# Updating the recurrent state of six heads behind the first output tiles of a two-layer step

## The chip, the cores and the metric

The kernel runs on one core of a Trainium2 chip. A core has five engines with an instruction queue each: TensorE (PE in the rows, with its weight loads as PEld), VectorE (DVE), ScalarE (ACT), GpSimd (POOL) and SyncE (SP, which here only issues DMAs). They are ordered among each other by semaphores. The metric is the device time of one launch in microseconds, the median of several runs.

## The reference

One step of a two-layer trunk for 256 prompt tokens and 8 sample tokens (each a sequence of its own with one new token). The first layer is sliding-window attention, the second a gated linear recurrence (HGRN2) with 12 heads of 128 x 128; both have four heads of attention on a memory, a gate, an output projection and a LayerNorm. What the change touches is the state of the sample tokens in the second layer, `state_hgrn`. With one token a sequence, the recurrence comes down to this, for each sample and head:

```python
fg = lb + (1.0 - lb) * sigmoid(f)      # 128 numbers, one per row of the state
k  = 1.0 - fg
state_new = fg[:, None] * state + k[:, None] * v[None, :]
o = q @ state_new                       # then RMS norm, gate, output projection
```

Both `o` and `state_new` are results: `o` feeds the rest of the layer, `state_new` is only stored (8 samples x 128 x 128 in float32, 512 KB a head).

## The kernel before

Tokens stand in columns, T = 264 of them (256 prompt, 8 sample). All large operands come through one list of **units**, built by `stream.add` and run by `Stream.run` (L58 to L131). A unit is one load of up to 128 x 2048 float32 (1 MB) on SP into a buffer `raw`, a split of it into two float16 parts `hl`, and a function that uses the split. The first part is rounded by ACT (L97), the remainder is made by DVE (L98), and every product is three PE passes (`passes`, L302 to L305). There are four `raw` and four `hl` buffers, used in turn; a unit's load waits until the raw slot that it takes has been released, its split until an hl slot has been. The last eight output tiles have hl buffers of their own, `held`, and are multiplied in two goes: first 176 columns, later the other 88.

For the second layer the list holds, for each pair of heads `pi`, the projections f and v of both heads, and then for each head the projection q, the state (`state_unit`) and, for the first eight heads, the gate (`early_gate`). Then come four projections `mq` for the memory's queries, four units of cached memory keys (`ck_unit`), four of cached memory values (`cv_unit`) with the gates 8 to 15 between them, and the sixteen tiles of the output weight `w_o` (`out_unit`). Gates 14 and 15 are the last two before the tiles. The prompt's recurrence (`hg_side`) and its memory attention (`memp_side`) are run in pieces between the units; the last head pair's norm (L1183, L1186) needs a logarithm and an exponential, with a load of ACT's tables ahead of each.

`state_unit(h)` computes o for the eight samples from the split state. It then updates the state in place in its raw slot: `sel` selects the value row of each sample on PE (`vb`, L1233), ACT scales the state by the forget gate (L1237), DVE adds the outer product (L1238), 8 of each for a head, and POOL issues the store (L1241). The unit is added with `whole=True`, so its raw slot stays taken until the unit is done, and the next load into it waits for the store.

A scheduler fixes the order on each engine; the order in which the functions are called is its input.

Of the kernel before, what the change touches and what calls it, by code (L numbers as in the profile page):

```python
# [18 lines left out]
P = 128  # L19
# [12 lines left out]
NM = 4  # L32
HD = 12
NG1 = 8
SW = 1024.0
SA = 8.0
SP = 1024.0
# [7 lines left out]
RMS_EPS = 1e-6  # L45
HALVES = ((0, slice(0, 64), slice(64, P)), (1, slice(64, P), slice(0, 64)))
LEVELS = (1, 2, 4, 8, 16, 32, 64)
NMASK = (len(LEVELS) - 1) * 64

SM_LB = 0  # L50
# [7 lines left out]
class Stream:  # L58
# [11 lines left out]

    def parts(self, i):
        n = 4 if i == 0 else 2 if i < 4 else 1
        w = self.units[i][0].shape[1] // n
        return [slice(k * w, (k + 1) * w) for k in range(n)]

    def load(self, i):
        t = self.pool.tile([P, 2048], F32, tag="raw", name=f"raw{i}", bufs=self.nraw)
        for k, s in enumerate(self.parts(i)):
            self.nc.sync.dma_start(t[:, s], self.units[i][0][:, s])
            if i < 4:  # L80
                self.after_load(i, k)
        self.raw[i] = t
# [52 lines left out]
def trunk_kernel(  # L135
# [73 lines left out]
    l_t = cp.tile([24, 383], F32, tag="ms", name="l_t", bufs=2)  # L209
    l_d = dp.tile([24, LROW], F32, name="l_d")[:, :]  # L210
    bias_s = pm.tile([P, 2, NQ], F32, name="bias_s")

    def small_work():
        with ExitStack() as behind:
# [695 lines left out]
    def wb(w, i):  # L910
        return w[i].rearrange("p c f -> p (c f)")
# [111 lines left out]
    def hv_unit(h):  # L1023
        def fn(hl):
            p1 = H["p"]
            i = h % 2
            pt = proj(hl, xhl, T, f"hv{h}")
            if i == 0:
                cur["vn"] = p1.tile([P, 2, 2, P], F32, tag="vn", name=f"vn{h}", bufs=2)
                cur["vr"] = p1.tile([P, 2, P], F16, tag="vr", name=f"vr{h}", bufs=2)  # L1030
                cur["vt"] = p1.tile([P, 2, T], F32, tag="vt", name=f"hvt{h}", bufs=1)
            vt = cur["vt"][:, i]
            vs = H["vs"][i]
            nc.scalar.activation(vt, pt, AF.Copy, scale=CP)
            split_from(vs[:, :TS], vs[:, TS : 2 * TS], pt[:, TP:T], 1.0 / SW)
            vn, vr = cur["vn"], cur["vr"]
            later.append(lambda: hv_rows(h, vt, vs, vn, vr))

        return fn

    def hv_rows(h, vt, vs, vn, vr):
        i = h % 2
        pt = bank("pt", 2, f"hvp{h}")
        for c in range(2):
            nc.tensor.transpose(pt[:, c * P : (c + 1) * P], vt[:, c * P : (c + 1) * P], ident)
        nc.scalar.activation(vn[:, i].rearrange("p c v -> p (c v)"), pt[:, :256], AF.Copy)
        p16 = ps.tile([P, P], F16, tag="pt", name=f"hvr{h}", bufs=2)
        nc.tensor.transpose(p16, vs, ident16)
        nc.vector.tensor_copy(vr[:, i], p16)

    def early_gate(j):
        def fn(hl):
# [11 lines left out]
    def hg_side(pi, q, vn, fg, qk):  # L1064
# [129 lines left out]
            done[1].add(h)  # L1194
        yield

    def state_unit(h):
        def fn(hl):
            p1 = H["p"]
            pi, i = h // 2, h % 2  # L1200
            raw = stream.raw[state_at[h]][:, : TS * P]
            R = raw.rearrange("p (b v) -> p b v", b=TS)
            v = hl[:, :, : TS * P].rearrange("p s (b v) -> p s b v", b=TS)
            vr, fgs, ks8 = cur["vr"][:, i], cur["fg"][:, i, TP:T], cur["ks8"][:, i]
            qs, vts = (cur[n][:, i, TP:T] for n in ("q", "vt"))
            ks = cur["kk"][:, i]
            if i == 0:
                osb[pi] = p1.tile([P, 2, T], F32, tag="osb", name=f"osb{pi}", bufs=2)
            qk = p1.tile([P, TS], F32, tag="qk", name=f"qk{h}", bufs=2)
            qf = p1.tile([P, TS], F32, tag="qf", name=f"qf{h}", bufs=2)  # L1210
            qfh = p1.tile([P, TS, 2], F16, tag="qfh", name=f"qfh{h}", bufs=2)
            nc.vector.scalar_tensor_tensor(qf, qs, SA * 0.5 * CP, fgs, op0=ALU.mult, op1=ALU.mult)
            nc.vector.scalar_tensor_tensor(qk, qs, 8.0 * 0.5 * CP / SK, ks, op0=ALU.mult, op1=ALU.mult)
            qkh = p1.tile([P, 2, TS], F16, tag="qkh", name=f"qkh{h}", bufs=2)
            nc.scalar.activation(qkh[:, 0], qk, AF.Copy)
            nc.vector.tensor_tensor(qkh[:, 1], qk, qkh[:, 0], op=ALU.subtract)
            nc.scalar.activation(qfh[:, :, 0], qf, AF.Copy)
            nc.vector.tensor_tensor(qfh[:, :, 1], qf, qfh[:, :, 0], op=ALU.subtract)
            po = bank("ms", 1, f"hos{h}")
            pov = po[:, : 2 * TS].rearrange("p (b s) -> p b s", s=2)  # L1220
            for b in range(TS):
                mm(pov[:, b], v[:, 0, b], qfh[:, b], start=True, stop=False)
                mm(pov[:, b, 0:1], v[:, 1, b], qfh[:, b, 0:1], start=False, stop=True)
            pq = po[:, 2 * TS : 3 * TS]
            for s in range(2):
                mm(pq, H["ones"], qkh[:, s], start=s == 0, stop=s == 1)
            nc.vector.tensor_reduce(qf, pov, axis=AX.X, op=ALU.add)
            nc.vector.tensor_tensor(qk, pq, vts, op=ALU.mult)
            nc.vector.scalar_tensor_tensor(osb[pi][:, i, TP:T], qf, 1.0 / (SA * SA), qk, op0=ALU.mult, op1=ALU.add)
            for g in range(2):  # L1230
                pvb = bank("pt", 2, f"vb{h}{g}")
                for bb in range(4):
                    mm(pvb[:, bb * P : (bb + 1) * P], H["sel"][:, 4 * g + bb], vr, start=True, stop=True)  # L1233
                for bb in range(4):
                    b = 4 * g + bb
                    s = R[:, b]
                    nc.scalar.activation(s, s, AF.Copy, scale=fgs[:, b : b + 1])  # L1237
                    nc.vector.scalar_tensor_tensor(  # L1238
                        s, pvb[:, bb * P : (bb + 1) * P], ks8[:, b : b + 1], s, op0=ALU.mult, op1=ALU.add
                    )  # L1240
            nc.gpsimd.dma_start(ss_o[pi, :, i * TS * P : (i + 1) * TS * P], raw)  # L1241

        return fn

    state_at = {}
    for pi in range(HD // 2):
        for part, unit in (("f", f_unit), ("v", hv_unit)):
            for i in range(2):
                stream.add(wb(w_in1, NB1[part] + 2 * pi + i), unit(2 * pi + i))
        for h in (2 * pi, 2 * pi + 1):  # L1250
            stream.add(wb(w_in1, NB1["q"] + h), hq_unit(h))
            state_at[h] = len(stream.units)
            stream.add(state[pi][:, (h % 2) * TS * P : (h % 2 + 1) * TS * P], state_unit(h), SA, whole=True)
            if h < NG1:
                stream.add(wb(w_in1, NB1["g"] + h), early_gate(h))
    for h in range(NM):
# [17 lines left out]
        g1(late.popleft())  # L1274
    for i in range(NC):
        stream.add(wb(w_o[1], i), out_unit(1, i), home=hold if i >= NC - NSPLIT else None)

    def after(i):
        if i == 1:
# [153 lines left out]
```

## Time and profile before

| | us |
|---|---|
| median of 3 runs | 905.26 |
| fastest and slowest | 904.99, 907.28 |
| profiled execution | 906.08 |
| its span in the profile | 904.3 |
| PE busy in the span | 886.6 |
| DVE busy | 701.5 |
| ACT busy | 582.4 |

The span runs from the first to the last recorded instruction; 1.78 us of the profiled execution lie around it. Busy times count instructions as they occupy an engine; transfers are not in them.

### The profile page before, as it was taken

Reading aid. Unit: us, or ns where it says so; the run is one execution under the profiler, and the core shown is the slowest. Engines: PE = TensorE matmul, PEld = TensorE weight load, DVE = VectorE, ACT = ScalarE, POOL = GpSimd, SP = SyncE. Lnnn points to the kernel's source line nnn. Section 1 sums busy time; section 2 is a strip of 40 time slices with the busy share of each in tenths; the row PEclk is TensorE's granted clock in tenths of the full one; section 3 lists DMA queues with packets and bytes.
Section 4 is the critical chain, followed back from the end, with each engine's and each line's share of the span. In section 5 each row is a group of like instructions: output and inputs, shape, how many; then the busy total and the mean of one; then the engine's idle time right before and its main releaser. Section 6 shows DMA issues by size and latency. Waiting matters only on the chain.

```text
span 904.3 us, 21814 instructions
## 1 busy us (share of the span) xinstructions
PE 886.6 (98%) x9281; PEld 762.9 (84%) x9281; DVE 701.5 (78%) x1230; ACT 582.4 (64%) x982; POOL 34.9 (4%) x68
## 2 busy tenths in 40 slices
PE   9999999999999999999999999999999999799996
PEld 6888889678888888876888888898888888688996
DVE  6879877669886666697687887979788989678736
ACT  6767776657664444476766877777777585858415
POOL 1100010000000000002000000000000000000000
PEclk9999999999999999999999999999999999899999
DMA  9998566557785555556374655827454878456303
GB/s 340 392 353 317 188 245 209 188 208 265 262 333 192 187 192 203 207 198 214 127 292 137 216 201 174 299 101 260 160 215 164 303 283 308 172 207 244 130 2 97
DMA packets 37853, 198.67 MB, mean 220 GB/s; under 512 B 4555, under 2 KB 10732, under 8 KB 17532
## 3 DMA queue, kind: packets, MB, share of 16 engines
q1 hardware_dynamic: 33024, 181.55, 56.3%
q0 software_dynamic: 4688, 15.67, 4.6%
q8 instruction: 72, 1.18, 0.5%
q14 instruction: 25, 0.20, 0.1%
q10 hardware_dynamic: 44, 0.07, 0.0%
HBM read 180.03 MB, written 17.22 MB: 218 GB/s over the span
## 4 chain that ended last, share of the span: by engine, by line
PE 77%; DVE 8%; ACT 6%; DMA 6%; issue 3%; SPq 0%; ACTq 0%; DVEq 0%
PE o L303 5%; PE o L305 5%; PE o L304 5%; PE g L305 5%; PE g L303 5%; PE g L304 5%; DVE hl L98 4%; ACT hl L97 2%; PE hv L305 2%; PE hv L303 2%; PE hv L304 2%; DMA raw<-in_w_in 2%; PE hq L303 2%; PE hq L305 2%; PE hq L304 2%
## 5 line engine op out<-in xcount | busy, mean ns | idle before, releaser
L98 DVE SCALAR_TENSOR_TENSOR hl<-raw,hl 128x2048 f16<-128x2048 f32 (+2 forms) x168 | 358.6, 2138 | 82.0 <-ACT hl L97 81.0
L97 ACT ACTIVATE hl<-raw 128x2048 f16<-128x2048 f32 (+2 forms) x168 | 299.2, 1784 | 97.8 <-PE o L305 45.4
L305 PEld LDWEIGHTS <-hl 128*128 128x128 f16 (+2 forms) x2048 | 197.4, 98 | 31.8 <-DVE hl L98 2.9
L303 PEld LDWEIGHTS <-hl 128*128 128x128 f16 (+2 forms) x2048 | 197.3, 98 | 30.6 <-issue 2.2
L304 PEld LDWEIGHTS <-hl 128*128 128x128 f16 (+2 forms) x2048 | 197.4, 98 | 30.3 <-issue 2.2
L305 PE MATMUL g<-xhl,hl 128*128 128x264 f16 x512 | 142.0, 277 | 2.4 <-DVE hl L98 2.4
L303 PE MATMUL g<-xhl,hl 128*128 128x264 f16 x512 | 141.9, 277 | 0.0
L304 PE MATMUL g<-xhl,hl 128*128 128x264 f16 x512 | 141.9, 277 | 0.0
L303 PE MATMUL o<-mix,hl 128*128 128x264 f16 x384 | 105.4, 276 | 0.8 <-DVE xres L747 0.8
L304 PE MATMUL o<-mix,hl 128*128 128x264 f16 x384 | 105.8, 276 | 0.0
L305 PE MATMUL o<-mix,hl 128*128 128x264 f16 x384 | 105.7, 276 | 0.0
L303 PE MATMUL q<-xhl,hl 128*128 128x264 f16 x192 | 53.0, 276 | 1.0 <-DVE kst L251 1.0
L303 PE MATMUL f<-xhl,hl 128*128 128x264 f16 x192 | 52.9, 276 | 0.4 <-DVE mvhl L251 0.4
L305 PE MATMUL hv<-xhl,hl 128*128 128x264 f16 x192 | 53.0, 276 | 0.0
L303 PE MATMUL hq<-xhl,hl 128*128 128x264 f16 x192 | 53.0, 276 | 0.0
L304 PE MATMUL hq<-xhl,hl 128*128 128x264 f16 x192 | 53.0, 276 | 0.0
L305 PE MATMUL hq<-xhl,hl 128*128 128x264 f16 x192 | 53.0, 276 | 0.0
L304 PE MATMUL hv<-xhl,hl 128*128 128x264 f16 x192 | 53.0, 276 | 0.0
L303 PE MATMUL hv<-xhl,hl 128*128 128x264 f16 x192 | 53.0, 276 | 0.0
L304 PE MATMUL q<-xhl,hl 128*128 128x264 f16 x192 | 53.0, 276 | 0.0
L305 PE MATMUL q<-xhl,hl 128*128 128x264 f16 x192 | 53.0, 276 | 0.0
L304 PE MATMUL f<-xhl,hl 128*128 128x264 f16 x192 | 52.9, 276 | 0.0
(338 smaller groups left out, 1858.4 us busy)
## 6 DMA issues: line engine op xcount, KB each, us to landing
raw<-in_w_in SPq DMA_DIRECT2D x88, 1024.0 KB, 6.4
raw<-in_w_o SPq DMA_DIRECT2D x32, 1024.0 KB, 5.0
raw<-in_w_mk SPq DMA_DIRECT2D x8, 1024.0 KB, 4.9
raw<-in_w_mv SPq DMA_DIRECT2D x8, 1024.0 KB, 4.9
raw<-in_c_mk SPq DMA_DIRECT2D x8, 1024.0 KB, 5.1
raw<-in_c_mv SPq DMA_DIRECT2D x8, 1024.0 KB, 7.0
raw<-in_state SPq DMA_DIRECT2D x12, 512.0 KB, 5.4
out_ss<-raw POOLq DMA_DIRECT2D x12, 512.0 KB, 5.5
```

Source lines behind the costliest of these rows:

```text
L97: hi = self.nc.scalar.activation(hl[:, 0, s], raw[:, s], AF.Copy, scale=scale)
L98: lo = self.nc.vector.scalar_tensor_tensor(hl[:, 1, s], raw[:, s], scale, hl[:, 0, s], op0=ALU.mult, op1=ALU.subtract)
L303: mm(out, lhs(0), rhs(0), start=start, stop=False)
L304: mm(out, lhs(0), rhs(1), start=False, stop=False)
L305: return mm(out, lhs(1), rhs(0), start=False, stop=stop)
```

## The change

The six heads of `LATER`, 6 to 11, leave their state alone in `state_unit`. Its end copies the forget gate and the scaled k of the eight samples behind the value rows in one small tile (`vr`, now 128 x 80 numbers a head) and stores it to DRAM, and the unit no longer keeps its raw slot. The update itself stands in new units, `update_unit(h)`, one behind each of the output tiles 0, 2, 4, 6, 8 and 10. Such a unit loads the state a second time, loads the small tile behind it into the same raw slot, is not split, and does the scales, sums and the store. The selector is loaded a second time, once, into a buffer that the memory softmax also uses. Nothing else changes.

```diff
--- before.py
+++ after.py
@@ -32,6 +32,7 @@
 NM = 4
 HD = 12
 NG1 = 8
+LATER = tuple(range(6, HD))
 SW = 1024.0
 SA = 8.0
 SP = 1024.0
@@ -45,6 +46,7 @@
 RMS_EPS = 1e-6
 HALVES = ((0, slice(0, 64), slice(64, P)), (1, slice(64, P), slice(0, 64)))
 LEVELS = (1, 2, 4, 8, 16, 32, 64)
+KEPT = P // 2 + 2 * TS
 NMASK = (len(LEVELS) - 1) * 64
 
 SM_LB = 0
@@ -70,12 +72,19 @@
 
     def parts(self, i):
         n = 4 if i == 0 else 2 if i < 4 else 1
-        w = self.units[i][0].shape[1] // n
+        src = self.units[i][0]
+        if isinstance(src, list):
+            return [None]
+        w = src.shape[1] // n
         return [slice(k * w, (k + 1) * w) for k in range(n)]
 
     def load(self, i):
         t = self.pool.tile([P, 2048], F32, tag="raw", name=f"raw{i}", bufs=self.nraw)
         for k, s in enumerate(self.parts(i)):
+            if s is None:
+                for home, src in self.units[i][0]:
+                    self.nc.sync.dma_start(home(t), src)
+                continue
             self.nc.sync.dma_start(t[:, s], self.units[i][0][:, s])
             if i < 4:
                 self.after_load(i, k)
@@ -209,6 +218,7 @@
     l_t = cp.tile([24, 383], F32, tag="ms", name="l_t", bufs=2)
     l_d = dp.tile([24, LROW], F32, name="l_d")[:, :]
     bias_s = pm.tile([P, 2, NQ], F32, name="bias_s")
+    kept = {pi: dp.tile([P, 2, KEPT], F32, name=f"kept{pi}") for pi in sorted({h // 2 for h in LATER})}
 
     def small_work():
         with ExitStack() as behind:
@@ -1027,7 +1037,7 @@
             pt = proj(hl, xhl, T, f"hv{h}")
             if i == 0:
                 cur["vn"] = p1.tile([P, 2, 2, P], F32, tag="vn", name=f"vn{h}", bufs=2)
-                cur["vr"] = p1.tile([P, 2, P], F16, tag="vr", name=f"vr{h}", bufs=2)
+                cur["vr"] = p1.tile([P, 2, KEPT], F32, tag="vr", name=f"vr{h}", bufs=2)
                 cur["vt"] = p1.tile([P, 2, T], F32, tag="vt", name=f"hvt{h}", bufs=1)
             vt = cur["vt"][:, i]
             vs = H["vs"][i]
@@ -1046,7 +1056,7 @@
         nc.scalar.activation(vn[:, i].rearrange("p c v -> p (c v)"), pt[:, :256], AF.Copy)
         p16 = ps.tile([P, P], F16, tag="pt", name=f"hvr{h}", bufs=2)
         nc.tensor.transpose(p16, vs, ident16)
-        nc.vector.tensor_copy(vr[:, i], p16)
+        nc.vector.tensor_copy(vr[:, i, : P // 2].bitcast(F16), p16)
 
     def early_gate(j):
         def fn(hl):
@@ -1194,6 +1204,33 @@
             done[1].add(h)
         yield
 
+    def update(h, R, vr, fgs, ks8, sel):
+        for g in range(2):
+            pvb = bank("pt", 2, f"vb{h}{g}")
+            for bb in range(4):
+                mm(pvb[:, bb * P : (bb + 1) * P], sel[:, 4 * g + bb], vr, start=True, stop=True)
+            for bb in range(4):
+                b = 4 * g + bb
+                s = R[:, b]
+                nc.scalar.activation(s, s, AF.Copy, scale=fgs[:, b : b + 1])
+                nc.vector.scalar_tensor_tensor(
+                    s, pvb[:, bb * P : (bb + 1) * P], ks8[:, b : b + 1], s, op0=ALU.mult, op1=ALU.add
+                )
+        nc.gpsimd.dma_start(ss_o[h // 2, :, h % 2 * TS * P : (h % 2 + 1) * TS * P], R.rearrange("p b v -> p (b v)"))
+
+    late_sel = []
+
+    def update_unit(h):
+        def fn(raw):
+            if not late_sel:
+                late_sel.append(cp.tile([P, TS, P], F16, tag="ms", name="late_sel", bufs=2))
+                nc.sync.dma_start(late_sel[0], sel_d)
+            R = raw[:, : TS * P].rearrange("p (b v) -> p b v", b=TS)
+            k = raw[:, TS * P : TS * P + KEPT]
+            update(h, R, k[:, : P // 2].bitcast(F16), k[:, P // 2 : P // 2 + TS], k[:, P // 2 + TS :], late_sel[0])
+
+        return fn
+
     def state_unit(h):
         def fn(hl):
             p1 = H["p"]
@@ -1201,7 +1238,7 @@
             raw = stream.raw[state_at[h]][:, : TS * P]
             R = raw.rearrange("p (b v) -> p b v", b=TS)
             v = hl[:, :, : TS * P].rearrange("p s (b v) -> p s b v", b=TS)
-            vr, fgs, ks8 = cur["vr"][:, i], cur["fg"][:, i, TP:T], cur["ks8"][:, i]
+            vr, fgs, ks8 = cur["vr"][:, i, : P // 2].bitcast(F16), cur["fg"][:, i, TP:T], cur["ks8"][:, i]
             qs, vts = (cur[n][:, i, TP:T] for n in ("q", "vt"))
             ks = cur["kk"][:, i]
             if i == 0:
@@ -1227,18 +1264,13 @@
             nc.vector.tensor_reduce(qf, pov, axis=AX.X, op=ALU.add)
             nc.vector.tensor_tensor(qk, pq, vts, op=ALU.mult)
             nc.vector.scalar_tensor_tensor(osb[pi][:, i, TP:T], qf, 1.0 / (SA * SA), qk, op0=ALU.mult, op1=ALU.add)
-            for g in range(2):
-                pvb = bank("pt", 2, f"vb{h}{g}")
-                for bb in range(4):
-                    mm(pvb[:, bb * P : (bb + 1) * P], H["sel"][:, 4 * g + bb], vr, start=True, stop=True)
-                for bb in range(4):
-                    b = 4 * g + bb
-                    s = R[:, b]
-                    nc.scalar.activation(s, s, AF.Copy, scale=fgs[:, b : b + 1])
-                    nc.vector.scalar_tensor_tensor(
-                        s, pvb[:, bb * P : (bb + 1) * P], ks8[:, b : b + 1], s, op0=ALU.mult, op1=ALU.add
-                    )
-            nc.gpsimd.dma_start(ss_o[pi, :, i * TS * P : (i + 1) * TS * P], raw)
+            if h in LATER:
+                tail = cur["vr"][:, i, P // 2 :]
+                nc.vector.tensor_copy(tail[:, :TS], fgs)
+                nc.vector.tensor_copy(tail[:, TS:], ks8)
+                nc.gpsimd.dma_start(kept[pi][:, i], cur["vr"][:, i])
+                return
+            update(h, R, vr, fgs, ks8, H["sel"])
 
         return fn
 
@@ -1250,7 +1282,7 @@
         for h in (2 * pi, 2 * pi + 1):
             stream.add(wb(w_in1, NB1["q"] + h), hq_unit(h))
             state_at[h] = len(stream.units)
-            stream.add(state[pi][:, (h % 2) * TS * P : (h % 2 + 1) * TS * P], state_unit(h), SA, whole=True)
+            stream.add(state[pi][:, (h % 2) * TS * P : (h % 2 + 1) * TS * P], state_unit(h), SA, whole=h not in LATER)
             if h < NG1:
                 stream.add(wb(w_in1, NB1["g"] + h), early_gate(h))
     for h in range(NM):
@@ -1274,6 +1306,13 @@
         g1(late.popleft())
     for i in range(NC):
         stream.add(wb(w_o[1], i), out_unit(1, i), home=hold if i >= NC - NSPLIT else None)
+        if i % 2 == 0 and i // 2 < len(LATER):
+            h = LATER[i // 2]
+            srcs = [
+                (lambda t: t[:, : TS * P], state[h // 2][:, (h % 2) * TS * P : (h % 2 + 1) * TS * P]),
+                (lambda t: t[:, TS * P : TS * P + KEPT], kept[h // 2][:, h % 2]),
+            ]
+            stream.add(srcs, update_unit(h), split=False)
 
     def after(i):
         if i == 1:
```

The first place is ACT's queue around the roundings of the last two value-cache units and gate 14. In the kernel before, hl152 and hl153 are the third and fourth value-cache units, hl154 is gate 14 and hl155 gate 15; `osb5` and `osq5` belong to the last head pair's norms, `sil` and `mix` to gates, `ms1` to the prompt's memory softmax, `msphl1` to the sample tokens' memory rows.

The rows before, with hl153 five and hl152 eight places above the first:

```order
L1173 ACTIVATE osb5_9734<-hpo5_10636 128x2x256
L1177 ACTIVATE osq50_10644<-osb5_9734 128x264
L1177 ACTIVATE osq51_10646<-osb5_9734 128x264
L249 ACTIVATE msphl1_10701<-mback1_10698 128x64
L1183 ACT_TABLE_LOAD
L1183 ACTIVATE osq50_10644<-rms50_10704,eps_rms_83 128x264
L1183 ACTIVATE osq51_10646<-rms51_10707,eps_rms_83 128x264
L1186 ACT_TABLE_LOAD
L1186 ACTIVATE osq50_10644<-osq50_10644 128x264
L1186 ACTIVATE osq51_10646<-osq51_10646 128x264
L97 ACTIVATE hl154_10975<-raw154_10717 128x2048
L729 ACTIVATE mix_95<-sil110_10630 128x264
```

Both value-cache units were rounded before all of these, and gate 14's rounding follows the norms' exponentials. In the changed kernel, with hl152 three places above the first row:

```order
L1193 ACT_TABLE_LOAD
L1193 ACTIVATE osq50_10503<-rms50_10563,eps_rms_83 128x264
L1193 ACTIVATE osq51_10505<-rms51_10566,eps_rms_83 128x264
L1196 ACT_TABLE_LOAD
L1196 ACTIVATE osq50_10503<-osq50_10503 128x264
L1196 ACTIVATE osq51_10505<-osq51_10505 128x264
L739 ACTIVATE mix_98<-sil110_10489 128x264
L739 ACTIVATE mix_98<-sil111_10627 128x264
L106 ACTIVATE hl153_10781<-raw153_10510 128x2048
L624 ACTIVATE ms10_10634,mz10_10636<-msc10_10633,mnm10_10635 128x256 x2
L624 ACTIVATE ms11_10765,mz11_10767<-msc11_10764,mnm11_10766 128x256 x2
L106 ACTIVATE hl154_10835<-raw154_10576 128x2048
```

The norms now stand ahead of the fourth value-cache unit, two gated heads' roundings and two pairs of softmax rows, and gate 14's rounding behind all of these.

The second place is ACT's queue before the roundings of the output tiles. hl160 is tile 4 before; in the changed kernel hl162 is tile 4, hl161 tile 3, and raw163 the third moved head's state. `mix_..<-sil115` is the rounding of gate 15, the last that the first output tiles need. Before:

```order
L733 ACTIVATE sil115_11292<-g115_11243 128x264
L729 ACTIVATE mix_95<-sil113_11029 128x264
L634 ACTIVATE mix_95<-mpo12_11097 128x256
L729 ACTIVATE mix_95<-sil114_11216 128x264
L634 ACTIVATE mix_95<-mpo13_11230 128x256
L729 ACTIVATE mix_95<-sil115_11292 128x264
L97 ACTIVATE hl160_11364<-raw160_11108 128x2048
L97 ACTIVATE hl161_11423<-raw161_11165 128x2048
```

After:

```order
L106 ACTIVATE hl161_11252<-raw161_11245 128x2048
L743 ACTIVATE sil115_11146<-g115_11097 128x264
L739 ACTIVATE mix_98<-sil113_10889 128x264
L644 ACTIVATE mix_98<-mpo12_10957 128x256
L739 ACTIVATE mix_98<-sil114_11072 128x264
L644 ACTIVATE mix_98<-mpo13_11086 128x256
L1215 ACTIVATE raw163_11249<-raw163_11249 128x128 x2
L739 ACTIVATE mix_98<-sil115_11146 128x264
L1215 ACTIVATE raw163_11249<-raw163_11249 128x128 x6
L106 ACTIVATE hl162_11309<-raw162_11247 128x2048
```

Eight scales of a reloaded state now stand around gate 15's rounding, two of them before it.

The third place is SP's queue with the loads of the first output tiles (raw156 is tile 0 in both). Before, one tile's load follows another:

```order
L79 DMA raw157_10925<-in_w_o 128x2048 [waits DMAHW6_49,DVE_49]
L79 DMA raw158_10978<-in_w_o 128x2048 [waits DMAHW7_49,DVE_49]
L79 DMA raw159_11055<-in_w_o 128x2048 [waits DMAHW0_49,DVE_49]
L79 DMA raw160_11108<-in_w_o 128x2048 [waits DMAHW1_49,DVE_49]
L79 DMA raw161_11165<-in_w_o 128x2048 [waits DMAHW2_49,DVE_49]
```

Each waits for the queue place of an earlier load (DMAHW) and for DVE's split of the unit whose slot it takes. After:

```order
L88 DMA raw156_10707<-in_w_o 128x2048 [waits DMAHW5_49,DVE_49]
L86 DMA raw157_10784<-in_state 128x1024 [waits DMAHW6_49,DVE_49]
L86 DMA raw157_10784<-kept3_93 128x80 [waits DMASW1_49]
L88 DMA raw158_10838<-in_w_o 128x2048 [waits DMAHW7_49,DVE_49]
L88 DMA raw159_10915<-in_w_o 128x2048 [waits DMAHW0_49,DVE_49]
L86 DMA raw160_10968<-in_state 128x1024 [waits DMAHW1_49,DVE_49]
L86 DMA raw160_10968<-kept3_93 128x80 [waits DMASW3_49]
L1227 DMA late_sel_11216<-in_sel 128x1024 [waits DVE_49,PE_49]
L88 DMA raw161_11245<-in_w_o 128x2048 [waits DMAHW4_49,DVE_49]
L88 DMA raw162_11247<-in_w_o 128x2048 [waits DMAHW5_49,DMAHW2_49,DVE_49]
L86 DMA raw163_11249<-in_state 128x1024 [waits DMAHW3_49,DMAHW1_49,DVE_49]
L86 DMA raw163_11249<-kept4_94 128x80 [waits DMASW4_49]
L88 DMA raw164_11393<-in_w_o 128x2048 [waits DMASW3_49,DVE_49,PE_49]
```

The moved heads' states and their small tiles now take two of every three or four places, with the second selector load among them, and wait for slots and for stores as well.

## Rows read from the trace of the kernel before

**Rows 1.** The page, busy time of each engine, share of the span, instructions.

```profile
PE 886.6 (98%) x9281; PEld 762.9 (84%) x9281; DVE 701.5 (78%) x1230; ACT 582.4 (64%) x982; POOL 34.9 (4%) x68
```

**Rows 2.** Windows of output tiles: span, busy (PE, PEld, DVE, ACT, POOL), PEclk, DMA share, GB/s.

```profile
820.00:840.00 20.00, 20.00 (x180) 17.39 (x178) 17.94 (x19) 14.23 (x11) 0.00 (x0) 1.00 0.92 339
850.00:870.00 20.00, 20.00 (x267) 20.00 (x265) 7.05 (x20) 2.17 (x6) 0.00 (x0) 1.00 0.01 2
```

**Rows 3.** A window of the heads stage, columns as in the group before.

```profile
640.00:660.00 20.00, 20.00 (x215) 17.88 (x214) 13.13 (x22) 14.74 (x37) 0.00 (x0) 1.00 0.23 86
```

**Rows 4.** Waits of PE from 735 to 904: total us, times, longest.

```profile
PE g L305 <- DVE hl L98: 2.4, 2, 1.7
PE hpo L1169 <- ACT st L1147: 1.5, 1, 1.5
PE mback L677 <- DVE mrows L674: 1.0, 1, 1.0
...
PE msc L303 <- ACT osq L1183: 0.4, 1, 0.4
PE hpo L1171 <- ACT s L1162: 0.3, 1, 0.3
```

**Rows 5.** Windows of 2 us between 778 and 788, columns as in rows 2.

```profile
778.00:780.00 2.00, 1.76 (x19) 1.31 (x19) 0.00 (x0) 1.97 (x4) 0.00 (x0) 0.53 0.05 21
780.00:782.00 2.00, 2.00 (x41) 1.68 (x40) 1.67 (x4) 2.00 (x3) 0.00 (x0) 0.61 0.03 8
784.00:786.00 2.00, 0.56 (x3) 0.43 (x4) 2.00 (x5) 2.00 (x3) 0.00 (x0) 0.74 0.00 0
786.00:788.00 2.00, 2.00 (x11) 1.36 (x10) 2.00 (x1) 2.00 (x6) 0.00 (x0) 0.50 0.64 201
```

**Rows 6.** Timeline of ACT, then PE, from 776 to 786.

```profile
776.17 0.22 ACT L249 ACTIVATE msphl<-mback 128x64 f16<-128x64 f32 x1
776.41 1.28 ACT L1183 ACT_TABLE_LOAD   x1
777.71 0.85 ACT L1183 ACTIVATE osq<-rms,eps_rms 128x264 f32<-128x264 f32 x2
778.58 1.28 ACT L1186 ACT_TABLE_LOAD   x1
779.87 0.73 ACT L1186 ACTIVATE osq<-osq 128x264 f32<-128x264 f32 x2
...
785.43 0.40 PE L305 MATMUL g<-xhl,hl 128*128 128x264 f16 x1 [1.73 <-DVE hl L98]
```

**Rows 7.** Instructions on tile raw: ns min/median/max, first and last start, forms.

```profile
L97 ACT ACTIVATE hl<-raw x168: 629/1902/1923, 3.7 to 829.2; 128x2048 f16<-128x2048 f32 x146, 128x1024 f16<-128x1024 f32 x18, 128x512 f16<-128x512 f32 x4
L98 DVE SCALAR_TENSOR_TENSOR hl<-raw,hl x168: 691/2291/2333, 4.4 to 831.9; 128x2048 f16<-128x2048 f32 x146, 128x1024 f16<-128x1024 f32 x18, 128x512 f16<-128x512 f32 x4
L1237 ACT ACTIVATE raw<-raw,fg x96: 384/390/402, 435.7 to 693.9; 128x128 f32<-128x128 f32 x96
L1238 DVE SCALAR_TENSOR_TENSOR raw<-vb,ks,raw x96: 340/344/352, 450.5 to 723.8; 128x128 f32<-128x128 f32 x96
```

**Rows 8.** Instructions on tile sel_t, columns as in the group before.

```profile
L1233 PE MATMUL vb<-vr,sel_t x96: 216/219/220, 450.1 to 722.3; 128*128 128x128 f16 x96
```

**Rows 9.** Timeline of the first output tiles, PE and ACT.

```profile
799.91 0.28 PE L303 MATMUL o<-mix,hl 128*128 128x264 f16 x1
...
811.19 0.42 ACT L729 ACTIVATE mix<-sil 128x264 f16<-128x264 f32 x1 [0.50 <-DVE sil L728]
...
814.62 0.27 PE L303 MATMUL o<-mix,hl 128*128 128x264 f16 x1 [0.30 <-DVE xres L747]
```

**Rows 10.** DMA issues: count, KB each, median us from issue to landing.

```profile
raw<-in_w_o SPq DMA_DIRECT2D x32, 1024.0 KB, 5.0
...
raw<-in_state SPq DMA_DIRECT2D x12, 512.0 KB, 5.4
out_ss<-raw POOLq DMA_DIRECT2D x12, 512.0 KB, 5.5
```

## The prediction

> **What bounds the kernel now.** The page comes first: PE is busy 98% of the span [rows 1], so a change can gain only where PE waits or runs at the low clock, and loses wherever it makes PE wait. The windows give PE's pace in the stage that receives work: 180 matmuls of 264 columns in 20 us are 0.111 us each, so a unit of 48 takes 5.36 us; 267 in 20 us are 0.075, so a unit on 176 columns takes 3.6 us [rows 2]. In the heads stage, from which work is taken, PE is full at full clock: 20.00 of 20 us, beside 13.13 of DVE and 14.74 of ACT [rows 3]. The sample states' scales and sums there take idle time of ACT and DVE.
>
> The waits of PE over the last 170 us then show where something is lost. Five of them lie between 763 and 791 us, where the memory attention of the second layer begins, and sum to 2.4 + 1.5 + 1.0 + 0.4 + 0.3 = 5.6 us [rows 4]. In the same place the granted clock falls: 0.53, 0.61, 0.74 and 0.50 in four stretches of 2 us [rows 5]. Against full clock these lose 2 x (0.47 + 0.39 + 0.26 + 0.50) = 3.2 us, of which about 0.4 lies in the idle time counted already, an estimate. The **hole** is worth about 8.4 us. Its cause reads off the timeline [rows 6]: ACT has two table loads of 1.28 us around the logs of the last head pair, then gate 14's rounding, and PE starts gate 14's last pass after 1.73 us of waiting, at 785.43. Until the memory rows are back, all four buffers of split units are held by the value-cache units, so no gate can be split ahead.
>
> **The change, part by part.**
>
> *Heads stage.* Of each of six heads 8 scales of 0.39 us go from ACT and 8 sums of 0.34 us from DVE [rows 7], 3.1 and 2.7 us by single durations, some 14 to 19 us an engine in all. They lie beside a full PE [rows 3]: worth 0 to the span there. The two small copies a head and the stores of 41 KB also lie under that PE time: 0. What does change is when the work behind them runs: in the new order the last head pair's last matmuls stand before gate 14 by some 110 matmuls more than before, 12 us, under gates 11 to 13. Hence the chance of filling the hole.
>
> *The hole afterwards.* I followed the new order by hand from the end of gate 12's matmuls (time 0), which frees the buffer for the third value-cache unit. ACT rounds it until 1.9 (1.902 [rows 7]); a gate's tanh and the memory rows' small copy, 0.22, end at 2.5; table load, logs, table load, exponentials, 1.28 + 0.85 + 1.28 + 0.73 = 4.1 [rows 6], end at 6.6; two gated heads' roundings wait for DVE's products and end at 9.2; only then the fourth value-cache unit is rounded, until 11.1; two pairs of softmax rows, about 0.9 a pair, end at 12.9. DVE finishes that unit 2.29 later, at 13.4, and with reductions and products before it gets to gate 14's remainder at 16.2 and ends at 18.4. PE's own content up to the point that needs it is 13.3: it waits 5.1, and 1.1 more behind the softmax rows, together 6.2. Thin PE work of about 9 us goes with this as it does in [rows 5]; a dip of the kind seen there costs 1.7 to 2.9 more. I take 8.0, with bounds 0 (the rounding of unit four slips ahead) and 9. Against 8.4: **-0.4**. The table loads and the splits stay in one chain on ACT, and it is only begun earlier.
>
> *Matmuls moved.* 48 of 0.22 us, four overlapped at 0.055 [rows 8]: 2.6 us, taken from one full stretch and put into another: 0.
>
> *First output tiles.* Times from the start of the first output matmul, before at 799.91 [rows 9]. The third tile began at 814.62, 14.7 later, with gate 15 rounded on ACT 11.3 after the start. The content is 96 output matmuls, 24 others and small waits, so only 1.1 of it was lost. Now the scales of the third moved head stand ahead of gate 15 on ACT, and they wait for a load. The load of that state needs a raw slot: two of four slots hold the first two moved heads, and the slot comes free when tile 3 has been split. I put tile 3's load behind the wait of the second selector load on SP, its split on ACT at +5.5 and on DVE at +8.1 (an estimate: 5.0 us to land [rows 10] and 1.9 and 2.3 to split [rows 7]). The state is then issued at +8.2 and lands 5.4 later [rows 10], at about +13.6; two scales and the rounding end at +14.8, the remainder at +15.2. PE wants it at about +12.4 (77 output matmuls, 12 others and 8 narrow ones make 10.3; small waits 2). The rest of tiles 0 and 1 follows, and tile 2 starts at +16.7 to +17.4 instead of +13.0: a wait of 3.7 to 4.4, less the 1.1 of before. I take **+3.2**, with bounds 0 (the load lands 4 us sooner) and 6 (tile 3 is late itself by the two units ahead of it).
>
> The Trainium skill bears on the stores: "DMA: Bandwidth & Descriptors", section "Anatomy of one DMA — SWDGE (gpsimd) path", fits such a transfer as 2.0 us plus its bytes at 436 GB/s, 3.2 us for half a megabyte; the rows here have 5.5 for these stores [rows 10], and the measurement decides. By the page the stores that release slots would end 2.3 us sooner, the tail below would be near 0.1, and the sum 2.3 lower.
>
> *Later output tiles.* Six extra units of half a megabyte take turns in the four slots, each held until its sums are done and its store of 5.5 us has landed [rows 10]. I followed the resolved order: tile 5's load waits for the first head's store, tile 7's for the second's, tiles 10, 11 and 14 for the next three; tile 13's waits for tile 11's split. Tiles 5 to 10 have 3 to 8 us to spare. Tile 11 is 0.3 late; its split ends at +62.3, tile 13 lands at +67.5, is split (1.9 + 2.3 [rows 7]) at +71.7 and was wanted at +69.6. So **+2.4**; bounds 0 (one store quicker by 2.4) and 6 (each of the last three tiles late by 2). The work itself, 2.3 us of ACT and 2.2 of DVE a unit when run back to back, lies under PE's 5.36.
>
> *Sum.* The profiled execution took 906.08 us: 906.08 - 0.4 + 3.2 + 2.4 = 911.3. It stands 0.82 above the median of 905.26, so 910.5 for the median.
>
> **The rivals.**
>
> *A, the hole closes.* Heads freed of 14 us on each engine let the last pair be ready early, the table loads run under gates 11 to 13, and gate 14 is split in time. For it: the memory rows now come some 12 us earlier in PE's order. Against it: the third and fourth value-cache units and both table loads still stand in a row on ACT before gate 14. If 6 to 8 of the 8.4 vanish and the output stage loses no more than 2 net, the time is 905.3 - 6 + 2 = 901, within 899 to 902 for the ends of these. This is the case on the other side; it decides if gate 14's remainder ends within 13.3 us of gate 12's end instead of 18.4.
>
> *B, it cancels.* The hole shrinks by 3 and the output stage loses 3, or neither moves, since the loads land in time: 902.6 to 907.9. For it: slots had time to spare at tiles 5 to 10.
>
> *C, the slots bind.* A reload that waits for a store, a store that waits for sums behind a load, and PE's clock at half after each wait as in [rows 5]: hole 8.4 stays, +6 and +6 with two dips of 1.7 less some overlap: 905.3 + 10 to 12 = 915 to 917. The Trainium skill's page "TensorE: Matmul & The Clock Gate", section "HAM oscillation — how this bites in real kernels", says that waits on transfers can drop the clock again and again; the windows after the waits agree, with 0.53 and 0.50. Against it: single waits of 0.3 to 2 us as before need not do that.
>
> **How the numbers follow.** Forecast, slower by 3 to 9 us: 0.43; A 0.22; B 0.23; C 0.12. A change of 0.3%, 2.7 us, is about what a measurement of this kernel can tell from none. Faster by more is A, 0.22; within it B, 0.23; slower the forecast and C, 0.55. The range reaches to A's 901 and C's 917; half of each may lie outside, under 0.2 together. The forecast's own range is 908 to 914: the sum with one of its two output terms at one of its bounds at a time (910.5 - 2.4 and 910.5 + 3.6).
>
> **What would show it.** Right: between gates 13 and 14 PE still waits for DVE's split, with windows at half clock; a wait of 3 to 4 us before tile 2, ended by gate 15's rounding on ACT behind scales of a reloaded state that themselves waited for their load; SP waiting for stores; waits of 1 to 2 us at tiles 11 and 13. Wrong: full PE windows from the heads to the first output tile at full clock (A), or scales of reloaded states that never wait (B). The weakest step is the hand-followed queue of ACT in the hole: one split earlier there moves the result by the whole width of A.

## The result, and the profile after

The changed kernel takes 910.22 us (median of 9 runs, 907.12 to 911.43) beside 905.99 for the kernel before on the same chips: a ratio of 1.0037, 95% interval 1.0022 to 1.0052, so slower by some 4 us, as forecast. Its profiled execution took 909.75 us, with a span of 908.0 against 904.3: 3.7 us more. The two halves of the sum did not come out as forecast.

PE's busy time on the page, beside [rows 1]:

```profile
PE 887.1 (98%) x9281; PEld 763.7 (84%) x9281; DVE 702.9 (77%) x1242; ACT 582.1 (64%) x982; POOL 38.3 (4%) x74
```

Two long windows split the gain from the loss (span, then busy us of PE, PEld, DVE, ACT, POOL, granted clock, DMA share, GB/s). First the changed kernel, then the kernel before:

```profile
400.00:800.00 400.00, 397.42 (x4149) 341.76 (x4148) 327.54 (x577) 282.91 (x463) 16.29 (x30) 0.99 0.58 207
800.00:880.00 80.00, 72.94 (x796) 67.17 (x795) 57.33 (x110) 40.06 (x64) 3.21 (x6) 1.00 0.63 223
```

```profile
400.00:800.00 400.00, 393.76 (x4142) 338.24 (x4140) 333.60 (x605) 287.41 (x486) 16.01 (x30) 0.99 0.61 216
800.00:880.00 80.00, 79.23 (x856) 72.85 (x855) 50.20 (x72) 36.46 (x44) 0.00 (x0) 1.00 0.35 131
```

Up to the output tiles PE is idle 3.7 us less; in the tiles it is idle 6.3 us more, while the DMA share goes from 0.35 to 0.63. The waits of PE from 735 us on (total us, times, longest) say the same, beside [rows 4]:

```profile
PE o L313 <- DVE xres L757: 7.0, 3, 2.9
PE g L315 <- DVE hl L107: 0.8, 1, 0.8
PE msc L313 <- ACT ms L624: 0.7, 1, 0.7
PE mso L706 <- ACT hl L106: 0.5, 1, 0.5
```

The hole's waits fell from 5.6 to 2.0 us. The clock did not follow them; windows of 2 us, beside [rows 5]:

```profile
774.00:776.00 2.00, 1.32 (x9) 0.89 (x9) 2.00 (x2) 2.00 (x9) 0.00 (x0) 0.82 0.03 8
776.00:778.00 2.00, 2.00 (x38) 1.67 (x37) 2.00 (x9) 2.00 (x3) 0.00 (x0) 0.50 0.41 121
778.00:780.00 2.00, 2.00 (x10) 1.58 (x8) 2.00 (x4) 2.00 (x2) 0.00 (x0) 0.50 0.48 162
780.00:782.00 2.00, 1.21 (x7) 0.82 (x7) 2.00 (x4) 2.00 (x5) 0.00 (x0) 0.50 0.27 33
782.00:784.00 2.00, 2.00 (x11) 1.38 (x10) 2.00 (x2) 2.00 (x10) 0.00 (x0) 0.50 0.77 279
784.00:786.00 2.00, 2.00 (x13) 1.46 (x12) 2.00 (x2) 2.00 (x9) 0.00 (x0) 0.62 0.97 397
```

Half clock, 1.2 of 2.4 GHz, is granted over 8 us after the thin stretch: 2 x (0.18 + 4 x 0.50 + 0.38) = 5.1 us lost against 3.2 before. Counted as the forecast did, the hole is worth some 6.7 us (2.0 + 5.1, less 0.4 in which both overlap, an estimate) against 8.4. This count is too high for the clock. In the window from 776 us 31 of the 38 matmuls are those of the sample tokens' memory attention, of one or two columns (the same window, tile `mso` alone):

```profile
776.00:778.00 2.00, 1.01 (x31) 0.00 (x0) 0.50 0.41 121
```

They start every 0.027 us there and every 0.025 at full clock, so half clock costs them next to nothing. By the starts of the matmuls, against the pace of the same kind at full clock, the stretch from 755 us to the first output matmul loses 10.0 us before (5.5 of it waits) and 7.1 after (2.0 waits), an estimate.

The timeline of PE, ACT and SP (its loads of tiles 3 and 4, then of the third moved state) at the two places of the prediction, beside [rows 6, 9]:

```profile
780.84 0.40 PE L315 MATMUL g<-xhl,hl 128*128 128x264 f16 x1 [0.79 <-DVE hl L107]
...
790.57 7.67 SPq L88 DMA_DIRECT2D raw<-in_w_o  x2
...
795.87 0.28 PE L313 MATMUL o<-mix,hl 128*128 128x264 f16 x1
...
801.40 0.33 SPq L86 DMA_DIRECT2D raw<-in_state  x1
...
805.41 0.69 ACT L1215 ACTIVATE raw<-raw 128x128 f32<-128x128 f32 x2 [2.27 <-DMA raw<-kept]
806.01 0.41 ACT L739 ACTIVATE mix<-sil 128x264 f16<-128x264 f32 x1
...
880.15 0.35 PE L813 MATMUL lnm<-acc,ones_ln 128*128 128x176 f32 x1
```

The first output matmul is 4.04 us earlier than before. Of that, 2.6 are the 48 narrow matmuls that now come later, and 19 matmuls of the memory attention, 2.1 us at 0.111, that ran between the first tiles before (by the counts of the two traces) now run ahead of them: the relief is 4.0 - 2.6 + 2.1 = 3.5. From the first output matmul to the first of the last norm it is 84.28 us against 77.17 (877.08 for the latter in the kernel before): +7.1, of which 2.6 - 2.1 is moved work and 6.6 is loss. The rest, 0.6, falls behind the norm. Gate 15's rounding does wait behind two scales of a reloaded state, which waited 2.27 us for a load, but it ends 10.5 us after the first output matmul, not 14.8, and no wait of PE stands at the third tile.

The 7.0 us are three waits, before tiles 9, 11 and 13. The timeline of ACT, DVE and PE at the first:

```profile
841.30 1.91 ACT L106 ACTIVATE held<-raw 128x2048 f16<-128x2048 f32 x1 [4.00 <-DMA raw<-in_w_o]
...
843.24 2.29 DVE L107 SCALAR_TENSOR_TENSOR held<-raw,held 128x2048 f16<-128x2048 f32 x1 [2.72 <-ACT held L106]
845.45 0.43 DVE L775 TENSOR_TENSOR acc<-acc,sq 128x264 f32<-128x264 f32 x1
845.81 2.29 DVE L107 SCALAR_TENSOR_TENSOR held<-raw,held 128x2048 f16<-128x2048 f32 x1
848.02 0.42 DVE L757 SCALAR_TENSOR_TENSOR xres<-xres,o 128x264 f32<-128x264 f32 x1
...
845.98 0.61 PE L1211 MATMUL vb<-raw,late_sel 128*128 128x128 f16 x8
848.49 0.24 PE L313 MATMUL o<-mix,held 128*128 128x176 f16 x1 [1.90 <-DVE xres L757]
```

ACT waits 4.00 us for tile 9's load, and its remainder on DVE is done at 845.5, in time for PE. But the remainder of the next tile follows at once, and the residual sum that empties a PSUM bank (the place where PE leaves its products) stands behind both in DVE's queue. PE waits for that bank: here a late load reaches PE by way of another tile's sum. At tiles 11 and 13 it reaches PE directly:

```profile
856.09 2.29 DVE L107 SCALAR_TENSOR_TENSOR held<-raw,held 128x2048 f16<-128x2048 f32 x1 [1.36 <-ACT held L106]
858.29 0.33 DVE L757 SCALAR_TENSOR_TENSOR xres<-xres,o 128x176 f32<-128x176 f32 x1
858.68 0.24 PE L313 MATMUL o<-mix,held 128*128 128x176 f16 x1 [2.23 <-DVE xres L757]
...
866.64 2.29 DVE L107 SCALAR_TENSOR_TENSOR held<-raw,held 128x2048 f16<-128x2048 f32 x1 [2.36 <-ACT held L106]
869.24 0.24 PE L313 MATMUL o<-mix,held 128*128 128x176 f16 x1 [2.92 <-DVE xres L757]
```

DVE itself waits for the rounding of the tile that PE wants, and that tile's remainder ends at 858.4 and 868.9, 0.3 us before PE goes on; the sum behind it adds no more than that. None of the three waits lowered the clock: it is 1.00 in the window from 800 to 880 us above.

### The profile page after: what moved, and what is told of

Same layout as the page of the kernel before. It is cut to its first block, busy times and chain, and to the rows that moved or that the text cites. A ratio compares the mean times of both kernels' runs of the same rounds, so it can differ in the third digit from the quotient of the medians.

```text
span 908.0 us, 21874 instructions
## 1 busy us (share of the span) xinstructions
PE 887.1 (98%) x9281; PEld 763.7 (84%) x9281; DVE 702.9 (77%) x1242; ACT 582.1 (64%) x982; POOL 38.3 (4%) x74
## 4 chain that ended last, share of the span: by engine, by line
PE 84%; DMA 6%; DVE 4%; ACT 4%; issue 1%; SPq 0%; ACTq 0%; DVEq 0%
PE g L315 6%; PE g L313 6%; PE g L314 6%; PE o L313 5%; PE o L315 5%; PE o L314 5%; DMA raw<-in_w_o 3%; PE q L313 2%; PE hv L313 2%; PE q L314 2%; PE q L315 2%; PE hv L314 2%; PE hv L315 2%; PE f L313 2%; PE f L315 2%; PE f L314 2%
## 5 line engine op out<-in xcount | busy, mean ns | idle before, releaser
L315 PEld LDWEIGHTS <-hl 128*128 128x128 f16 (+2 forms) x2048 | 197.6, 98 | 30.3 <-DVE hl L107 1.2
```

What stands on the lines that cost most here:

```text
L315: return mm(out, lhs(1), rhs(0), start=False, stop=stop)
```

## Experiments

Three theories of the loss in the tiles: **S**, the reloads hold raw slots and make the tiles' loads late; **W**, the scales and sums stand in the way on ACT and DVE; **T**, the added bytes slow the loads. Each run was timed in five rounds beside the kernel before (906.21 to 906.57). The expectations put the changed kernel's waits in the tiles at 6.5 us; the rows above give 7.0.

**The relief alone.** The units are not added, and heads 6 to 11 are not updated.

```diff
-        if i % 2 == 0 and i // 2 < len(LATER):
...
-            stream.add(srcs, update_unit(h), split=False)
```

> The update of heads 6 to 11 is left out altogether (no matmuls, scales, sums, reload or store; the small stores of what it would need stay). What is left of the change is the relief of the heads stage. If the relief itself is worth about 2 us in the hole and at the third tile, 906.0 - 2.6 (matmuls) - 1.9 = 901.5. Rival, the hole gains nothing and only the matmuls go: 903.4. It is the base from which the other kernels' costs are counted.

897.39 us, ratio 0.9902 [0.9883, 0.9921]: 9.2 less than before, 4 less than expected. With 2.6 for the matmuls, the relief is worth about 6.6 by the medians (by the spans, 895.5 and 904.3, 6.2); it was expected at 1.9.

**The work without a slot**, at the same places (ahead of tiles 1, 3, ... 11):

```diff
+            if l == 1 and i % 2 == 1 and i // 2 < len(LATER):
+                update_small(LATER[i // 2])
...
+                s = cp.tile([P, P], F32, tag="mrows", name=f"one{h}{b}")
+                nc.scalar.activation(s, pvb[:, bb * P : (bb + 1) * P], AF.Copy, scale=fgs[:, b : b + 1])
...
-            stream.add(srcs, update_unit(h), split=False)
```

> The six moved updates' matmuls, scales and sums are done behind tiles 1, 3, 5, 7, 9 and 11 on a small buffer, with no second load of the state, no raw slot and no store (the new state of heads 6 to 11 is left out; the work has the same instructions and sizes). S: no waits at the tiles: before's time less 1.4 in the hole and less 0.5 at the third tile, 903 to 905. W: the waits stay, 908 to 910.

900.91 us, 0.9935 [0.9917, 0.9952]. All of PE's waits after 735 us:

```profile
PE g L315 <- DVE hl L107: 0.8, 1, 0.8
PE msc L313 <- ACT ms L624: 0.7, 1, 0.7
PE mso L706 <- ACT hl L106: 0.5, 1, 0.5
```

None stands at a tile. The work costs 3.5 over the run before this, of which the matmuls are 2.6. W falls. What is left of the changed kernel's time, 910.2 - 900.9 = 9.3, belongs to reloading, slots and stores.

**The slot without the work:**

```diff
-        for g in range(2):
+        for g in range(0 if h in LATER else 2):
```

> The six moved updates keep their second load, their raw slot and their store, but their matmuls, scales and sums are left out (the stored state of heads 6 to 11 is the old one). The changed kernel waits 6.5 us at output tiles 9, 11 and 13. Theory S (the reloads' hold on raw slots makes the tiles' loads late): only the 48 matmuls go, 2.6 us, and perhaps 1 to 2 us of hold: 905.5 to 907.6. Theory W (scales and sums stand among the splits and residual sums on ACT and DVE and make them late): the waits go too, 901 to 902.

907.76 us, 1.0009 [0.9994, 1.0023], no change from before that can be told, 0.2 above S's range and far from W's. The waits, of PE from 735 us and of ACT from 795 to 880:

```profile
PE o L313 <- DVE xres L757: 6.1, 1, 6.1
```

```profile
ACT held L106 <- DMA raw<-in_w_o: 20.1, 7, 10.0
```

PE still loses 6.1 us, now at one place, behind a residual sum that stands behind tile 8's late split in DVE's queue, and ACT waits 20.1 us for the last eight tiles' loads (11.6 in the changed kernel). The cost over the relief alone is 10.4 us, with no work in it. This one long wait also brought half clock, as the three shorter ones did not; two windows of 2 us behind it:

```profile
830.00:832.00 2.00, 1.61 (x8) 1.10 (x8) 2.00 (x2) 1.57 (x2) 0.00 (x0) 0.50 1.22 277
832.00:834.00 2.00, 2.00 (x11) 1.34 (x10) 2.00 (x4) 0.65 (x1) 0.00 (x0) 0.50 0.68 258
```

**The slot without the store:**

```diff
+        if h not in LATER:
             nc.gpsimd.dma_start(ss_o[...], R...)
```

> The six moved updates are done but not stored (the new state of heads 6 to 11 is left out of the output), so their raw slots come free at the last sum, some 4 us sooner than with the store. S: the loads behind them start sooner and most of the 6.5 us of waits goes: 904.5 to 907. W: nothing about ACT and DVE changes: 909.5 to 910.5.

905.15 us, 0.9988 [0.9973, 1.0002]: 5 less than the changed kernel. PE's wait for residual sums falls from 7.0 to 3.1 us. The store that ends a slot's turn carries about half of the loss, by its hold on the slot or by its bytes: the edit takes away both.

**The bytes without a slot**, two tries that tell nothing about T. The first sent the state through a small buffer that the work also used:

```diff
+            t = cp.tile([P, 2 * P], F32, tag="mrows", name=f"dead{h}{q}")
+            nc.gpsimd.dma_start(t, state[h // 2][:, at : at + 2 * P])
+            nc.gpsimd.dma_start(ss_o[h // 2, :, at : at + 2 * P], t)
```

> As the work without a slot, but for each of the six heads the state is also loaded a second time and stored, in quarters through a small buffer on POOL's queue, so the bytes of the change move and no raw slot is held (the stored state of heads 6 to 11 is the old one). S (slots): 901 to 903. Rival T (the added bytes slow the tiles' loads, whatever buffer they land in): 907 to 910.

1000.55 us, 1.1042 [1.1017, 1.1066]. The edit made a wait of its own: work and transfers took turns in one buffer, and the narrow matmuls waited for it.

```profile
PE vb L1243 <- DVE one L1248: 61.8, 6, 24.7
```

The second copied from DRAM to DRAM:

```diff
+        nc.gpsimd.dma_start(ss_o[h // 2, :, own], state[h // 2][:, own])
```

> As the work without a slot, but each head's old state is also copied from its place in DRAM to the output on POOL's queue beside its update, 512 KB read and 512 KB written a head as in the change, with no buffer on the chip in between (the stored state of heads 6 to 11 is the old one). S (slots): 901 to 903. T (the added bytes slow the tiles' loads): 906 to 910.

916.95 us, 1.0117 [1.0097, 1.0137], by POOL's timeline for another reason:

```profile
3.34 3.12 POOL L1235 DMA_DIRECT2D out_ss<-in_state  x6
```

The copies depend on nothing and were issued at 3.34 us, among the kernel's first loads. There the time was lost: in the first 80 us PE is busy 70.7 us at a granted clock of 0.87, against 77.0 at 1.00 before. They met no output tile.

**The slots with few bytes.** Same units, places, matmuls, scales and sums; an eighth of the load and of the store.

```diff
-                (lambda t: t[:, : TS * P], state[h // 2][...]),
+                (lambda t: t[:, 7 * P : TS * P], state[h // 2][... + 7 * P : ...]),
...
-                nc.scalar.activation(s, s, AF.Copy, scale=fgs[:, b : b + 1])
+                nc.scalar.activation(s, R[:, 7] if h in LATER else s, AF.Copy, scale=fgs[:, b : b + 1])
```

> The changed kernel with the same units in the same places, the same matmuls, scales and sums, but of each reloaded state only one sample's eighth (64 KB) is loaded and stored; the scales of the other samples read that eighth, and seven eighths of the new state of heads 6 to 11 are not stored. The raw slots are held from the load to the store as before, with an eighth of the bytes. S (the held slot and its chain of load, sums, store): the waits at tiles 9 to 13 stay for the most part, less some 2 us a turn for shorter loads and stores: 906 to 909. T (the bytes): the waits go, 901 to 903.

902.06 us, 0.9954 [0.994, 0.9967]: where T put it. S as stated, a slot held whatever its transfers, falls. The DMA issues of this run (KB each, median us to landing, over a whole run: half of the `w_o` loads are the first layer's, and in the changed kernel 12 of the 18 state loads and 6 of the 12 stores are the heads stage's), then of the changed kernel:

```profile
raw<-in_w_o SPq DMA_DIRECT2D x32, 1024.0 KB, 4.9
...
raw<-in_state SPq DMA_DIRECT2D x6, 64.0 KB, 2.0
out_ss<-raw POOLq DMA_DIRECT2D x6, 64.0 KB, 1.9
```

```profile
raw<-in_w_o SPq DMA_DIRECT2D x32, 1024.0 KB, 5.3
raw<-in_state SPq DMA_DIRECT2D x18, 512.0 KB, 4.5
...
out_ss<-raw POOLq DMA_DIRECT2D x12, 512.0 KB, 4.0
```

A slot's turn is shorter by (4.5 - 2.0) + (4.0 - 1.9) = 4.6 us in transfers, and tiles' loads land 0.4 sooner. The totals do not part the two. The times at which SP sends the loads say more; those of tiles 9 and 10, in the changed kernel, then in this run:

```profile
835.65 1.93 SPq L88 DMA_DIRECT2D raw<-in_w_o  x2
```

```profile
830.29 2.80 SPq L88 DMA_DIRECT2D raw<-in_w_o  x2
```

Counted from the first output matmul, tile 9's load goes out at +39.8 in the changed kernel, at +34.9 here and at +18.4 in the work without a slot, and is on its way for 5.6, 5.8 and 4.8 us. Tile 13's goes out at +62.5, +55.5 and +30.3 and takes 6.3, 5.1 and 5.9 us. So the loads are late because they are sent late, when a slot comes free; that the bytes slow a load on its way, which is T, makes 0.8 and 0.4 us of it. With few bytes the turns are shorter, and tiles are sent 5 to 7 us sooner than in the changed kernel, which is enough. The next three groups of runs move all the bytes (or those of some heads) and change turns and places.

**Behind the last tile**, four heads one by one, or three pairs, each pair in one slot:

```diff
-        if i % 2 == 0 and i // 2 < len(LATER):
+        for h in LATER if i == NC - 1 else ():
```

```diff
+        for pi in kept if i == NC - 1 else ():
+            stream.add([(lambda t: t, state[pi])], update_pair(pi), split=False)
```

> Only heads 8 to 11 are moved, and all four updates stand behind tile 15, when the raw slots are no longer wanted by tiles. S: no waits at tiles 9 to 13; if four heads give most of the relief, 901 to 904. Rival E (scales and sums now stand beside the last norms on ACT and DVE and delay the end): 905 to 909.

> All six heads are moved; each pair's state is loaded as one unit of 1 MB into one raw slot, the small tiles of all pairs into a buffer of their own, and the three units stand behind tile 15. S: 901 to 903, that is the work without a slot plus up to 2 at the end. E: 905 to 909.

908.26 (1.0021 [1.0007, 1.0034]) and 910.61 (1.0046 [1.0032, 1.0059]). With the pairs the tiles run without a wait: the last norm's first matmul is at 869.74, 10.4 earlier than in the changed kernel, 2.6 of it the updates' own matmuls. But the order on PE puts the updates' matmuls behind nearly all others, where nothing covers them, and with two PSUM banks they wait for DVE's sums:

```profile
PE vb L1211 <- DVE raw L1216: 7.7, 8, 2.4
```

So E was right about the first total, 1.6 too low for the second, and not by delaying the norms: a new wait at the end.

**Pairs at the old places** (behind tiles 0, 4 and 8):

```diff
+        for pi in [list(kept)[i // 4]] if i in (0, 4, 8) else ():
```

> As the pairs, but the three units stand behind tiles 0, 4 and 8, so that half as many slots are taken for the same bytes and the same work at about the same places. S: about half of the 8 us that the slots cost comes back, 904 to 907. T: same bytes, 908 to 910.

909.00 us, 1.0035 [1.0018, 1.0052], out of S's range and where T put it. The waits tell why:

```profile
PE o L313 <- DVE xres L757: 2.5, 3, 1.5
PE o L313 <- ACT mix L739: 2.0, 2, 1.5
...
PE vb L1211 <- DVE raw L1216: 1.1, 2, 0.7
```

With half the turns and all the bytes the waits for residual sums fall from 7.0 to 2.5 us, but new ones come: two gates' roundings behind a pair's scales on ACT (2.0, the kind of wait that the prediction put at the third tile), and the narrow matmuls for sums.

**Pairs late** (behind tiles 9, 11 and 13, the second head one tile later), and **the last pair alone** (behind tile 11):

```diff
+        for pi in [list(kept)[(i - 9) // 2]] if i in (9, 11, 13) else []:
...
+            one(2 * pi)
+            second.append(lambda: one(2 * pi + 1))
```

```diff
-LATER = tuple(range(6, HD))
+LATER = tuple(range(10, HD))
...
+        for pi in kept if i == 11 else []:
```

> All six heads, each pair in one raw slot, with the units behind tiles 9, 11 and 13 and the second head of each done behind the next tile, where the tiles' loads are 20 us ahead in the kernel without updates. S: no waits for loads at the tiles and no queue of narrow matmuls at the end: 901 to 903, faster than before. Rival: a slot held from its early load on makes the last four tiles late whatever its place: 905 to 910.

> Only heads 10 and 11 are moved, as one unit of 1 MB in one raw slot behind tile 11. If the relief comes from the last pair alone (what stands right before the hole), and S holds: 901.5 to 903.5. If it comes from all six heads: 904.5 to 906.

904.19 us, 0.9975 [0.9964, 0.9986], and 900.46, 0.9933 [0.9913, 0.9953]: both faster than the kernel before, the first 1.2 above the range of S, the second 1.0 below that of the last pair. The waits of PE at the tiles with the pairs late:

```profile
PE o L313 <- DVE xres L757: 1.1, 1, 1.1
PE vb L1213 <- DVE raw L1218: 0.9, 2, 0.5
```

The same bytes as in the changed kernel leave 2.0 us of waits in half the turns and where tiles are loaded ahead, against 7.0. The last pair alone has no wait at a tile, and its window from 840 to 880 us is full:

```profile
840.00:880.00 40.00, 40.00 (x562) 39.21 (x560) 23.53 (x48) 9.72 (x17) 0.54 (x1) 1.00 0.12 44
```

By the medians it is 5.9 us faster than before although only two heads left the heads stage, so nearly all the relief would come from the pair next to the hole. The traces do not show that much: the six executions lie between 898.85 and 903.31 us, the profiled one is the slowest, its span is 2.8 below that of before, and PE still waits 2.2 us for gate 14's remainder.

## Why the prediction was right in its sum and not in its parts

- *Heads stage, 0; matmuls, 0.* Right: the 48 matmuls cost as much in one stretch as in the other, and the work on ACT and DVE is nearly free (3.5 us, 2.6 of them matmuls).
- *The hole, -0.4.* Mis-sized, on both sides. The queues of ACT and DVE were followed rightly: gate 14's remainder ends 17.8 us after ACT took up the third value-cache unit (762.99 to 780.8), forecast 18.4, and PE's work up to there is 13.1 at the pace of full clock (an estimate), forecast 13.3. That PE waits only 0.8 for it and not 5.1 is because half clock stretched that work to 15.8 and 1.2 of waits stand before it. With the dip behind it the hole now costs about 7 us, forecast 8.0; the 1.1 behind the softmax rows lies inside the 5.1 and was counted twice. The larger miss is the hole before, 10.0 by the starts of the matmuls and not 8.4. What went away are the waits of the last pair and of the memory rows (`hpo` and `mback` in [rows 4], 2.8 us). Counted by the first output matmul the relief is 3.5; in the kernel without the updates it is 5.1 by the same count and 6.2 by the whole span. Rival A's gain came by about half, but its condition, the remainder within 13.3 us, did not.
- *First output tiles, +3.2.* This step failed. It put tile 3's load at about -1.4 against the first output matmul (a split at +5.5 less 5.0 and 1.9); the load was issued at 790.57, 5.3 before it. So the third moved state was asked for at +5.5 and not +8.2, its first scale ran at +9.5 where +13.6 was forecast, and gate 15 was rounded before PE asked. The mechanism exists: with pairs at the old places it costs 2.0.
- *Later tiles, +2.4.* The mechanism was right (turns of slots that end with a store; without the store 7.0 falls to 3.1), its size was not: 7.0. The splits came near where the forecast had them, counted from the first output matmul: tile 11's remainder ended at +62.5 (forecast +62.3), tile 13's at +73.1 (+71.7). But PE had lost nothing at the third tile and wanted tile 11 at +60.6, not at +62.0; it lost 2.2 there and 2.9 at tile 13. The other 1.9, at tile 9, I missed: I asked of each tile whether its own split was in time, and did not follow the residual sum behind two splits in DVE's queue.
- *Rival C.* Its dips did not come in the changed kernel, with waits of 1.9 to 2.9 us; the slot without the work, with one of 6.1, has one.
- *The sum.* In place of -0.4 + 3.2 + 2.4 = 5.2 the spans show -3.5 + 6.6 + 0.6 = 3.7. The relief was put too small by 3.1 us and the loss by 1.6. That these errors cancel in part is luck. That the two output terms come near the loss together is less so: they hang on one chain of slots, and what PE did not wait for at the third tile it waited for later.

On the stores: the Trainium skill's page "DMA: Bandwidth & Descriptors", section "Anatomy of one DMA — SWDGE (gpsimd) path", gives by its fit (2.0 us plus bytes at 436 GB/s) an estimate of 2.15 us for 64 KB, where the slots with few bytes show 1.9, and of 3.2 for 512 KB, where the changed kernel shows a median of 4.0; both lie below the 5.5 that the prediction took from [rows 10].

What stays open: how much of a turn's length is the update's own load and store and how much their sharing of the DMA engines with the tiles' loads. That slots and not slower loads make the tiles late rests on the times at which loads are sent. A kernel with all the bytes in the same places and no slot was not had: the two tries met other waits.

## What to carry to other kernels

Work that is free on a busy engine's neighbours is not free if it takes a buffer that the busy engine's loads pass through: count a moved step by the turn of its slot, load to store, not by its instructions. Try first to move only what stands next to the wait that it is to relieve; here, by the medians, two heads gave the gain of six. When a load comes late, look also for what stands behind it in the in-order queue of the engine that uses it, since PE may wait for that and not for the late tile (1.9 us at tile 9, 6.1 in the slot without the work).

## What was not expected

Fewer waits did not bring the clock back: with 2.0 us of waits in the hole in place of 5.6, half clock was granted for 8 us in a row, while PE is busy 2.00 of 2 us in three of these four windows, in the first of them mostly with matmuls of one or two columns. And six reloads and six stores cut to 64 KB each, with every turn of a slot kept, leave a kernel 4.4 us faster than the one before (906.45 in that run), where the changed kernel is 4 us slower.
